# Row skewness of a 1024 x 8192 matrix: part of the cubes on GpSimd, squares in PSUM from block 5 on, new unit sizes

## The chip, the cores and the metric

The kernel runs on one NeuronCore of a Trainium2 chip. The metric is the device time of one launch in microseconds (us). Five engines work side by side, each through its own queue in order: TensorE (PE; PEld is its weight load), VectorE (DVE), ScalarE (ACT), GpSimd (POOL) and SyncE (SP), which here issues the transfers. SBUF is the working memory of 128 partitions; PSUM is the smaller memory into which TensorE writes.

## The reference: the third standardized moment of each row

```python
mean = np.mean(x, axis=-1, keepdims=True)
std = np.std(x, axis=-1, keepdims=True)
z = (x - mean) / (std + 1e-8)
return np.mean(z ** 3, axis=-1).astype(np.float32)
```

x has 1024 rows of 8192 float32 values, 33.55 MB. The kernel reads it once and takes, for each row, the sums of x, of x squared and of x cubed. With m1, m2 and m3 the means of the three, the variance is m2 - m1^2, and the result is (m3 - 3 m1 m2 + 2 m1^3) times the variance to the power -1.5. It is computed as (m3 - 3 m1 (variance + m1^2 / 3)) times that power.

## The kernel before: how the work is cut and ordered

**Tiling.** The rows are 8 blocks (b from 0 to 7), each of one row per partition. The 8192 columns of a block are cut into units, which the table `UNITS` lists; (7,3) below is unit 3 of block 7. Each unit is one transfer (L130) into one of 8 buffers of the pool "xp", whatever its width. There are 31 units. The transfer of a unit waits until the unit eight places earlier has been read by all who read it.

**What is done with a unit.**
- Plain sums: TensorE transposes the unit in chunks of 128 columns and adds all chunks of a block up in one PSUM tile `tp` (L134). At the end of a block, ScalarE copies `tp` to SBUF as `tsb` (L164, for the last block L140), and a matmul with a column of 1/8192 (L165) adds up the 128 partitions, which gives the block's 128 row means, in column b of the PSUM tile `s1ps`.
- Squares: ScalarE squares a slice of the unit and its accumulator gives the slice's sum of squares (L146; in the profile a row ACTIVATE and a short row ACTIVATION_READ_ACCUMULATOR). The squares go to SBUF (pool "sqp", 4 buffers). From unit `PSUM_FROM` = (6,5) on they go to PSUM (pool "psq", 2 buffers).
- Cubes: VectorE multiplies the squares by x and its accumulator gives the sum of cubes (L150). Where the squares lie in SBUF, the product overwrites them. Where they lie in PSUM, it goes to one scratch tile `cube` that all such instructions share.

**Closing.** Blocks 0 to 6 are closed while block 7 is still being worked on, after the unit `EARLY_AT` = (7,2): ScalarE copies the means out of PSUM (L157) and takes three small functions of them (L113 to L115), VectorE adds up the slices' sums (L108), GpSimd does six small steps (L117 to L122). Block 7 is closed at the end: ScalarE copies `tp` (L140) before it squares the last unit, TensorE makes the means (L165), GpSimd and ScalarE take the variance and its power (L172 to L177, the power is L175), VectorE adds up the cubes (L178), joins (L179, L182), and one transfer writes the result (L183).

**Order.** The schedule is manual: each engine executes its instructions in the order in which the code above issues them. Waits between engines follow from the tiles that instructions read and write; an instruction that reads a tile of PSUM written by an earlier one waits for it. Nothing reorders a queue.

Of the kernel before, what the change touches and what calls it, by code (L numbers as in the profile page):

```python
# [8 lines left out]
FP = mybir.dt.float32  # L9
AF = mybir.ActivationFunctionType  # L10
ALU = mybir.AluOpType
# [3 lines left out]
UNITS = [  # L15
    [4096, 4096],
    [4096, 4096],
    [3456, 1792, 2944],
    [2944, 2304, 2944],
    [2944, 2688, 2560],  # L20
    [1920, 1920, 1792, 1536, 1024],
    [1536, 1408, 1408, 1152, 1408, 1280],
    [1152, 1280, 1408, 1280, 1280, 1280, 512],
]
PSUM_FROM = (6, 5)
SUB_MAX = 2304
PS_MAX, PS_BUFS = 1536, 2
X_BUFS = 8
SQ_BUFS = 4
EARLY = 7  # L30
EARLY_AT = (7, 2)


def _slices(w, most):
    n = -(-w // most)
    step = -(-w // n // 128) * 128
    return [(s, min(s + step, w)) for s in range(0, w, step)]


def _plan(b, k):  # L40
    return _slices(UNITS[b][k], PS_MAX if (b, k) >= PSUM_FROM else SUB_MAX)


@with_exitstack
def kernel(
    ctx: ExitStack,
    tc: tile.TileContext,
    x: bass.AP,
    out: bass.AP,
):  # L50
    nc = tc.nc
    eng = mybir.EngineType
    ctx.enter_context(tc.manual_schedule(
        engines={eng.PE, eng.Activation, eng.DVE, eng.Pool, eng.SP}))
    P = nc.NUM_PARTITIONS
    R, C = x.shape
    NB = R // P
    L = NB - 1
    F = EARLY
    inv_n = 1.0 / float(C)  # L60
    s_scale = float(C) ** -0.5
    third = (1.0 / 3.0) ** 0.5
    assert len(UNITS) == NB and all(sum(u) == C for u in UNITS) and F == L


    xv = x.rearrange("(p b) c -> b p c", b=NB)
    ov = out.rearrange("(p b) -> p b", b=NB)


    n_sl = [sum(len(_plan(b, k)) for k in range(len(u))) for b, u in enumerate(UNITS)]  # L70
    K = max(n_sl)

    xpool = ctx.enter_context(tc.tile_pool(name="xp", bufs=X_BUFS))
    sqpool = ctx.enter_context(tc.tile_pool(name="sqp", bufs=SQ_BUFS))
    onep = ctx.enter_context(tc.tile_pool(name="onep", bufs=1))
    psq = ctx.enter_context(tc.tile_pool(name="psq", bufs=PS_BUFS, space=bass.MemoryType.PSUM))
    psum1 = ctx.enter_context(tc.tile_pool(name="ps1", bufs=1, space=bass.MemoryType.PSUM))

    def small(name, n):
        return onep.tile([P, n], FP, tag=name, name=name)  # L80

    onesn = small("onesn", 1)
    nc.vector.memset(onesn, inv_n)  # L83
    tiny = small("tiny", 1)
    nc.scalar.activation(out=tiny, in_=onesn, func=AF.Square)  # L85
    ident = small("ident", P)
    make_identity(nc, ident)
    s2u = small("s2u", NB * K)
    s3u = small("s3u", NB * K)
    nc.vector.memset(s2u, 0.0)  # L90
    nc.vector.memset(s3u, 0.0)
    cube = small("cube", PS_MAX)
    junk = small("junk", K)
    expo = small("expo", F)
    nc.gpsimd.memset(expo, -1.5)
    skew = small("skew", NB)
    m1a = small("m1a", F)
    tsb = small("tsb", P)

    tp = psum1.tile([P, P], FP, tag="tp", name="tp")  # L100
    s1ps = psum1.tile([P, NB], FP, tag="s1ps", name="s1ps")
    act, g = nc.scalar.activation, nc.gpsimd

    def close_first_blocks():

        m2, m3 = small("m2a", F), small("m3a", F)
        for dst, src in ((m2, s2u), (m3, s3u)):
            nc.vector.tensor_reduce(  # L108
                out=dst, in_=src[:, 0 : F * K].rearrange("p (b c) -> p b c", c=K),
                axis=X_AXIS, op=ALU.add,  # L110
            )
        m1sq, m1sq3, nm1 = small("m1sqa", F), small("m1sq3a", F), small("nm1a", F)
        act(out=m1sq, in_=m1a, func=AF.Square)  # L113
        act(out=m1sq3, in_=m1a, func=AF.Square, scale=third)
        act(out=nm1, in_=m1a, func=AF.Copy, scale=-3.0)  # L115
        var, rr = small("vara", F), small("rra", F)
        g.tensor_tensor(out=var, in0=m2, in1=m1sq, op=ALU.subtract)  # L117
        g.tensor_tensor(out=m1sq3, in0=m1sq3, in1=var, op=ALU.add)
        g.tensor_tensor(out=m1sq3, in0=m1sq3, in1=nm1, op=ALU.mult)
        g.tensor_tensor(out=m3, in0=m3, in1=m1sq3, op=ALU.add)  # L120
        g.tensor_tensor(out=rr, in0=var, in1=expo, op=ALU.pow)  # L121
        g.tensor_tensor(out=skew[:, 0:F], in0=m3, in1=rr, op=ALU.mult)  # L122

    for b, widths in enumerate(UNITS):
        c0 = 0
        j = b * K
        for k, w in enumerate(widths):
            last_unit = b == L and k == len(widths) - 1
            xt = xpool.tile([P, w], FP, tag="x", name=f"x_{b}_{k}")
            nc.sync.dma_start(out=xt, in_=xv[b, :, c0 : c0 + w])  # L130
            c0 += w
            n = w // P
            for c in range(n):
                nc.tensor.matmul(  # L134
                    out=tp, lhsT=xt[:, c * P : (c + 1) * P], rhs=ident,
                    start=(k == 0 and c == 0), stop=(c0 == C and c == n - 1),
                    is_transpose=True,
                )
            if last_unit:
                nc.scalar.copy(out=tsb, in_=tp)  # L140
            for s, e in _plan(b, k):
                if (b, k) >= PSUM_FROM:
                    sq = psq.tile([P, PS_MAX], FP, tag="psq", name=f"psq_{b}_{k}_{s}")[:, 0 : e - s]
                else:
                    sq = sqpool.tile([P, e - s], FP, tag="sq", name=f"sq_{b}_{k}_{s}")
                act(  # L146
                    out=sq, in_=xt[:, s:e], func=AF.Square, scale=s_scale,
                    accum_out=s2u[:, j : j + 1],
                )
                nc.vector.scalar_tensor_tensor(  # L150
                    out=cube[:, 0 : e - s] if (b, k) >= PSUM_FROM else sq,
                    in0=sq, scalar=1.0, in1=xt[:, s:e],
                    op0=ALU.mult, op1=ALU.mult, accum_out=s3u[:, j : j + 1],
                )
                j += 1
            if (b, k) == EARLY_AT:
                nc.scalar.copy(out=m1a, in_=s1ps[:, 0:F])  # L157
                close_first_blocks()
            if b == L and k == len(widths) - 2:
                m2p = small("m2p", 1)  # L160
                act(out=junk[:, 0 : n_sl[L] - 1], in_=s2u[:, L * K : j], func=AF.Copy,
                    accum_out=m2p)
        if b < L:
            nc.scalar.copy(out=tsb, in_=tp)  # L164
        nc.tensor.matmul(out=s1ps[:, b : b + 1], lhsT=tsb, rhs=onesn, start=True, stop=True)  # L165


    p1 = s1ps[:, L : L + 1]
    m1sq, nm1, v3, m2, var, rr, num = (
        small(f"{t}_l", 1) for t in ("m1sq", "nm1", "v3", "m2", "var", "rr", "num")  # L170
    )
    g.tensor_tensor(out=m2, in0=m2p, in1=s2u[:, j - 1 : j], op=ALU.add)  # L172
    act(out=m1sq, in_=p1, func=AF.Square)
    g.tensor_tensor(out=var, in0=m2, in1=m1sq, op=ALU.subtract)  # L174
    g.tensor_tensor(out=rr, in0=var, in1=expo[:, 0:1], op=ALU.pow)  # L175
    act(out=nm1, in_=p1, func=AF.Copy, scale=-3.0)
    act(out=v3, in_=m1sq, func=AF.Identity, scale=1.0 / 3.0, bias=var)  # L177
    nc.vector.tensor_reduce(out=num, in_=s3u[:, L * K : L * K + n_sl[L]], axis=X_AXIS, op=ALU.add)  # L178
    nc.vector.scalar_tensor_tensor(  # L179
        out=num, in0=v3, scalar=nm1, in1=num, op0=ALU.mult, op1=ALU.add  # L180
    )
    nc.vector.tensor_tensor(out=skew[:, L:NB], in0=num, in1=rr, op=ALU.mult)  # L182
    nc.sync.dma_start(out=ov, in_=skew)  # L183
# [30 lines left out]
```

## Time and profile before

| what | us |
|---|---|
| median of 3 runs (lowest and highest) | 92.29 (92.27 to 92.38) |
| the profiled execution | 92.38 |
| its span, first to last instruction | 90.6 |
| VectorE busy | 74.1 |
| ScalarE busy | 69.1 |
| TensorE busy | 66.5 |
| GpSimd busy | 4.2 |

The difference between the profiled execution's time and its span, 1.8 us, lies around the span. A row of the profile gives the engine, the line, the operation, output and inputs by the program's names, the shapes, and times in us (a mean in ns). In brackets stands the idle time of the engine just before, and who ended it. A matmul's end is modelled; successive transposes overlap. The granted TensorE clock of the core was 0.99.

### The profile page before, as it was taken

How to read it: one execution, taken by the hardware profiler on the slowest of the kernel's cores; microseconds unless marked ns; L12 is line 12 of the kernel's file. 1: busy time of each engine (PE TensorE's matmuls, PEld its weight loads, DVE VectorE, ACT ScalarE, POOL GpSimd, SP SyncE). 2: the span in 40 equal slices, each digit the busy share in tenths (PEclk: the TensorE clock that was granted, in tenths of full speed). 3: DMA queues.
4: the chain of work that ended last, by engine and by line, in shares of the span. 5: the costliest groups of instructions: out<-in, count | busy, mean ns of one | idle time of the engine just before them, and what ended most of it. 6: DMA issues, size and time to landing. Idle time of an engine off the chain costs nothing. (4 is left out here: it accounts for less than half of the span.)

```text
span 90.6 us, 1442 instructions
## 1 busy us (share of the span) xinstructions
PE 66.5 (73%) x528; PEld 60.2 (66%) x528; DVE 74.1 (82%) x92; ACT 69.1 (76%) x103; POOL 4.2 (5%) x16
## 2 busy tenths in 40 slices
PE   0003999988986959897589778989898798897700
PEld 0003999887975949686569667978687586776600
DVE  0000498969999799999988999999999989989980
ACT  6003969497885979897589889989888798898910
POOL 3000000000000000000000000000000000006440
PEclk9999999999999999999999999999999999999996
DMA  3999999999999999999999999999999999992000
GB/s 101 347 412 427 441 427 420 434 449 430 397 407 442 419 432 426 420 428 418 422 421 433 411 426 411 409 410 420 411 416 420 409 411 421 412 397 115 0 0 2
DMA packets 4614, 33.64 MB, mean 371 GB/s; under 512 B 640, under 2 KB 640, under 8 KB 3072
## 3 DMA queue, kind: packets, MB, share of 16 engines
q1 hardware_dynamic: 4608, 33.56, 89.4%
q8 instruction: 4, 0.07, 0.3%
q14 instruction: 2, 0.02, 0.0%
HBM read 33.55 MB, written 0.00 MB: 370 GB/s over the span
## 5 line engine op out<-in xcount | busy, mean ns | idle before, releaser
L134 PE MATMUL tp<-ident,x 128*128 128x128 f32 x512 | 64.0, 282 | 16.0 <-DMA x<-in_x_dram 15.8
L150 DVE SCALAR_TENSOR_TENSOR sq<-sq,x 128x2048 f32<-128x2048 f32 (+9 forms) x34 | 62.0, 1872 | 12.4 <-ACT sq L146 12.3
L134 PEld LDWEIGHTS tp<-ident,x 128*128 128x128 f32 x512 | 58.3, 146 | 20.3 <-DMA x<-in_x_dram 11.9
L146 ACT ACTIVATE sq<-x 128x2048 f32<-128x2048 f32 (+9 forms) x34 | 53.5, 1575 | 14.4 <-DMA x<-in_x_dram 12.6
L150 DVE SCALAR_TENSOR_TENSOR cube<-psq,x 128x1280 f32<-128x1280 f32 (+3 forms) x8 | 11.1, 1390 | 0.7 <-ACT psq L146 0.2
L146 ACT ACTIVATE psq<-x 128x1280 f32<-128x1280 f32 (+3 forms) x8 | 9.3, 1161 | 0.9 <-DVE cube L150 0.5
L146 ACT ACTIVATION_READ_ACCUMULATOR sq<-x 128x1 f32 x34 | 6.3, 186 | 0.0
L165 PEld LDWEIGHTS s1ps<-onesn,tsb 128*128 128x128 f32 x16 | 2.4, 188 | 5.2 <-ACT tsb L164 4.7
L165 PE MATMUL s1ps<-onesn,tsb 128*128 128x1 f32 x16 | 3.1, 260 | 3.4 <-ACT tsb L164 3.0
L117 POOL TENSOR_TENSOR vara<-m2a,m1sqa 128x7 f32<-128x7 f32 x1 | 0.2, 206 | 80.8 <-DVE m3a L108 80.8
L150 DVE DVE_READ_ACCUMULATOR sq<-sq,x 128x1 f32 x34 | 2.8, 82 | 0.0
L164 ACT COPY tsb<-tp 128x128 f32<-128x128 f32 x7 | 1.7, 250 | 1.3 <-PE tp L134 1.2
L85 ACT ACT_TABLE_LOAD x1 | 1.3, 1283 | 0.7 <-PEq L198 0.7
L121 POOL TENSOR_TENSOR rra<-vara,expo 128x7 f32<-128x7 f32 x1 | 1.5, 1507 | 0.0
L146 ACT ACTIVATION_READ_ACCUMULATOR psq<-x 128x1 f32 x8 | 1.5, 188 | 0.0
L83 DVE MEMSET onesn<- 128x1 f32 x1 | 0.1, 59 | 0.8 <-PEq L198 0.8
L150 DVE DVE_READ_ACCUMULATOR cube<-psq,x 128x1 f32 x8 | 0.7, 84 | 0.0
L177 ACT ACTIVATE v_l<-m1sq_l,var_l 128x1 f32<-128x1 f32 x1 | 0.3, 294 | 0.4 <-POOL var_l L174 0.4
L175 POOL TENSOR_TENSOR rr_l<-var_l,expo 128x1 f32<-128x1 f32 x1 | 0.6, 563 | 0.1
L179 DVE SCALAR_TENSOR_TENSOR num_l<-v_l,nm_l,num_l 128x1 f32<-128x1 f32 x1 | 0.2, 220 | 0.1
masks.py:199 POOL TENSOR_SCALAR_AFFINE_SELECT ident<-ident 128x128 f32<-128x128 f32 x1 | 0.3, 294 | 0.1
L140 ACT COPY tsb<-tp 128x128 f32<-128x128 f32 x1 | 0.3, 266 | 0.0
(27 smaller groups left out, 4.5 us busy)
## 6 DMA issues: line engine op xcount, KB each, us to landing
x<-in_x_dram SPq DMA_DIRECT2D x4, 2048.0 KB, 14.1
x<-in_x_dram SPq DMA_DIRECT2D x4, 1472.0 KB, 27.2
x<-in_x_dram SPq DMA_DIRECT2D x5, 640.0 KB, 9.3
x<-in_x_dram SPq DMA_DIRECT2D x4, 704.0 KB, 10.1
x<-in_x_dram SPq DMA_DIRECT2D x2, 960.0 KB, 19.8
x<-in_x_dram SPq DMA_DIRECT2D x2, 896.0 KB, 22.6
x<-in_x_dram SPq DMA_DIRECT2D x1, 1728.0 KB, 25.4
x<-in_x_dram SPq DMA_DIRECT2D x2, 768.0 KB, 15.2
```

The lines of the kernel that those rows point to most:

```text
L85: nc.scalar.activation(out=tiny, in_=onesn, func=AF.Square)
L117: g.tensor_tensor(out=var, in0=m2, in1=m1sq, op=ALU.subtract)
L121: g.tensor_tensor(out=rr, in0=var, in1=expo, op=ALU.pow)
L134: nc.tensor.matmul(out=tp, lhsT=xt[:, c * P : (c + 1) * P], rhs=ident, start=(k == 0 and c == 0), stop=(c0 == C and c == n - 1), is_transp ...
L140: nc.scalar.copy(out=tsb, in_=tp)
L146: act(out=sq, in_=xt[:, s:e], func=AF.Square, scale=s_scale, accum_out=s2u[:, j : j + 1],)
L150: nc.vector.scalar_tensor_tensor(out=cube[:, 0 : e - s] if (b, k) >= PSUM_FROM else sq, in0=sq, scalar=1.0, in1=xt[:, s:e], op0=ALU.mult, ...
L164: nc.scalar.copy(out=tsb, in_=tp)
L165: nc.tensor.matmul(out=s1ps[:, b : b + 1], lhsT=tsb, rhs=onesn, start=True, stop=True)
L175: g.tensor_tensor(out=rr, in0=var, in1=expo[:, 0:1], op=ALU.pow)
L177: act(out=v3, in_=m1sq, func=AF.Identity, scale=1.0 / 3.0, bias=var)
L179: nc.vector.scalar_tensor_tensor(out=num, in0=v3, scalar=nm1, in1=num, op0=ALU.mult, op1=ALU.add)
```

## The change

Five things change together.

- `UNITS` is cut anew, still 31 units: block 2 gets two large units, block 7 gets nine units, seven of 1024 to 896 columns and then 768 and 384.
- The first 1024 columns of the units (6,0), (7,0) and (7,2) get their cubes from GpSimd (`POOL`). (7,0) and (7,2) are 1024 columns wide and are done wholly there; of (6,0), 512 columns stay on VectorE. ScalarE squares into a tile `gsq` in SBUF (2 buffers), and GpSimd multiplies it by x in place.
- GpSimd's product has no accumulator here, so the cubes are added up as the plain sums are, by the new `sum_cubes`: TensorE transposes eight chunks into one PSUM tile, ScalarE copies it to SBUF, a matmul with a column of ones follows, and ScalarE copies the result into the slice's place in `s3u`. The three steps are issued after the third, fourth and fifth unit that follow.
- Squares go to PSUM from unit (5,3) on, in slices of at most 1024 columns and with 3 buffers, instead of from (6,5) on with at most 1536 and 2.
- The PSUM tile `s1ps` becomes a part of a tile `misc`, which also holds the transposed cubes (`gps`) and their sums. `EARLY_AT` is now (7,3). In the built program, the copy of the means (in the old code L157) waits until TensorE has finished the transposes of the cubes of (7,0), which are issued just before it.

```diff
 UNITS = [
     [4096, 4096],
     [4096, 4096],
-    [3456, 1792, 2944],
-    [2944, 2304, 2944],
-    [2944, 2688, 2560],
-    [1920, 1920, 1792, 1536, 1024],
-    [1536, 1408, 1408, 1152, 1408, 1280],
-    [1152, 1280, 1408, 1280, 1280, 1280, 512],
+    [4096, 4096],
+    [3584, 2560, 2048],
+    [3072, 2816, 2304],
+    [2816, 1664, 2176, 1536],
+    [1536, 1920, 1920, 1024, 896, 896],
+    [1024, 1024, 1024, 1024, 1024, 1024, 896, 768, 384],
 ]
-PSUM_FROM = (6, 5)
+POOL = {(6, 0): 1024, (7, 0): 1024, (7, 2): 1024}
+PSUM_FROM = (5, 3)
 SUB_MAX = 2304
-PS_MAX, PS_BUFS = 1536, 2
+PS_MAX, PS_BUFS = 1024, 3
...
-EARLY_AT = (7, 2)
+EARLY_AT = (7, 3)
...
 def _plan(b, k):
-    return _slices(UNITS[b][k], PS_MAX if (b, k) >= PSUM_FROM else SUB_MAX)
+
+    w, g = UNITS[b][k], POOL.get((b, k), 0)
+    most = PS_MAX if (b, k) >= PSUM_FROM else SUB_MAX
+    return ([(0, g, True)] if g else []) + [(g + s, g + e, False) for s, e in _slices(w - g, most)]
...
+    gpool = ctx.enter_context(tc.tile_pool(name="gp", bufs=2))
...
+    ones = small("ones", 1)
+    nc.gpsimd.memset(ones, 1.0)
...
+    gsb = small("gsb", P)
...
-    s1ps = psum1.tile([P, NB], FP, tag="s1ps", name="s1ps")
+    misc = psum1.tile([P, 2 * P], FP, tag="misc", name="misc")
+    gps = misc[:, 0:P]
+    s1ps = misc[:, P : P + NB]
...
+    def sum_cubes(sq, col):
+
+        n = sq.shape[1] // P
+        for c in range(n):
+            nc.tensor.matmul(
+                out=gps, lhsT=sq[:, c * P : (c + 1) * P], rhs=ident,
+                start=c == 0, stop=c == n - 1, is_transpose=True,
+            )
+        yield
+        nc.scalar.copy(out=gsb, in_=gps)
+        p3 = misc[:, P + NB : P + NB + 1]
+        nc.tensor.matmul(out=p3, lhsT=gsb, rhs=ones, start=True, stop=True)
+        yield
+        nc.scalar.copy(out=s3u[:, col : col + 1], in_=p3)
...
-            for s, e in _plan(b, k):
-                if (b, k) >= PSUM_FROM:
+            for s, e, on_pool in _plan(b, k):
+                if on_pool:
+                    sq = gpool.tile([P, e - s], FP, tag="gsq", name=f"gsq_{b}_{k}")
+                elif (b, k) >= PSUM_FROM:
...
-                nc.vector.scalar_tensor_tensor(
-                    out=cube[:, 0 : e - s] if (b, k) >= PSUM_FROM else sq,
-                    in0=sq, scalar=1.0, in1=xt[:, s:e],
-                    op0=ALU.mult, op1=ALU.mult, accum_out=s3u[:, j : j + 1],
-                )
+                if on_pool:
+                    g.tensor_tensor(out=sq, in0=sq, in1=xt[:, s:e], op=ALU.mult)
+                    steps = sum_cubes(sq, j)
+                    later += [(i + 3, steps), (i + 4, steps), (i + 5, steps)]
+                else:
+                    nc.vector.scalar_tensor_tensor(
+                        out=cube[:, 0 : e - s] if (b, k) >= PSUM_FROM else sq,
+                        in0=sq, scalar=1.0, in1=xt[:, s:e],
+                        op0=ALU.mult, op1=ALU.mult, accum_out=s3u[:, j : j + 1],
+                    )
                 j += 1
+            for at, steps in later:
+                if at == i:
+                    next(steps, None)
+            later = [z for z in later if z[0] > i]
             if (b, k) == EARLY_AT:
                 nc.scalar.copy(out=m1a, in_=s1ps[:, 0:F])
                 close_first_blocks()
...
+            i += 1
```

Here i counts units through all blocks, so the steps for (7,0) come after (7,3), (7,4) and (7,5), and those for (7,2) after (7,5), (7,6) and (7,7).

## The prediction

> **What bounds the kernel now.** I read the page first: engine shares, then its slices.
>
> ```profile
> span 90.6 us, 1442 instructions
> PE 66.5 (73%) x528; PEld 60.2 (66%) x528; DVE 74.1 (82%) x92; ACT 69.1 (76%) x103; POOL 4.2 (5%) x16
> ...
> PEclk9999999999999999999999999999999999999996
> DMA  3999999999999999999999999999999999992000
> ```
>
> The DMA row is what fills the span: its slices stand at 9 up to about 81 us, while no engine is busy for more than 82%. Loading sets the pace. TensorE's clock is full throughout. So what can be won or lost lies in how long the work goes on after the transfers, in the last ten us. The second view is the chain that ended last, in order of time; it names the engine that finishes last.
>
> ```profile
> 86.80 0.71 DVE cube L150 x2
> 87.51 0.02 issue
> 87.54 0.17 DVE num_l L178
> ...
> 88.14 0.16 DVE skew L182
> ```
>
> The chain is VectorE's alone. The third view is the timeline of the last ten us (start, duration, engine, line, operation; in brackets the idle time before it).
>
> ```profile
> 80.14 0.14 ACT L157 COPY m1a<-s1ps 128x7 f32<-128x7 f32 x1
> 80.31 1.31 PE L134 MATMUL tp<-ident,x 128*128 128x128 f32 x10 [0.17 <-DMA x<-in_x_dram]
> 80.62 1.22 ACT L146 ACTIVATE psq<-x 128x1280 f32<-128x1280 f32 x1
> 82.04 1.48 DVE L150 SCALAR_TENSOR_TENSOR cube<-psq,x 128x1280 f32<-128x1280 f32 x1
> 83.41 1.75 PE L134 MATMUL tp<-ident,x 128*128 128x128 f32 x14 [0.23 <-DMA x<-in_x_dram]
> 83.62 1.49 DVE L150 SCALAR_TENSOR_TENSOR cube<-psq,x 128x1280 f32<-128x1280 f32 x1
> 85.19 0.27 ACT L140 COPY tsb<-tp 128x128 f32<-128x128 f32 x1
> 85.21 1.49 DVE L150 SCALAR_TENSOR_TENSOR cube<-psq,x 128x1280 f32<-128x1280 f32 x1
> 85.36 0.61 ACT L146 ACTIVATE psq<-x 128x512 f32<-128x512 f32 x1
> 85.51 0.30 PEld L165 LDWEIGHTS s1ps<-onesn,tsb 128*128 128x128 f32 x2 [0.59 <-ACT tsb L140]
> 85.98 0.16 ACT L173 ACTIVATE m1sq_l<-s1ps 128x1 f32<-128x1 f32 x1
> 86.70 0.56 POOL L175 TENSOR_TENSOR rr_l<-var_l,expo 128x1 f32<-128x1 f32 x1
> 86.80 0.69 DVE L150 SCALAR_TENSOR_TENSOR cube<-psq,x 128x512 f32<-128x512 f32 x1
> 88.14 0.16 DVE L182 TENSOR_TENSOR skew<-num_l,rr_l 128x1 f32<-128x1 f32 x1
> ```
>
> VectorE takes one 1280-column cube every 1.58 to 1.59 us (82.04, 83.62, 85.21, 86.80), as long as such a unit takes to arrive (TensorE started on them at 80.31 and 83.41: two units in 3.10). It is about a unit behind and cannot catch up. A second path ends earlier: the copy of the sums at 85.19, the matmul, ScalarE's square at 85.98, GpSimd's steps, the power done at 86.70 + 0.56 = 87.26. The last operation, at 88.14, could have taken it 0.88 us sooner. So VectorE decides, with 0.88 us of room before the copy at 85.19 would.
>
> **The change part by part.**
>
> *Transfers.* 31 before and after, same bytes. In these rows a unit of 1280 columns takes 1.55 to 1.59 us, 1.21 to 1.24 us per 1000. I take the landing of any given column as unmoved by the new cuts. Unit (7,3) leaves 4096 columns to come; in the kernel before, unit (7,3), where TensorE starts at 80.31, leaves 3072. The 1024 columns between are 1.24 to 1.27 us: TensorE starts on the new (7,3) at 79.0. On SyncE's queue two transfers now wait for a GpSimd cube before their buffer is free, that of (7,2) for (6,0) and the last one for (7,0), whose end I put at 79.1 at the latest; the first transfer of all, issued at 0.74, let TensorE start at 8.29 with 4096 columns, so one of 384 needs some 3 us (7.55 less 3712 columns at 1.22), and it is wanted at 84. Hidden until GpSimd ends after 81.
>
> *VectorE.* It loses 3072 columns, 1.04 ns each (the 1408- and 512-column rows, 1625 and 691 ns, differ by 934 over 896): 3.2 us. Squares in PSUM cost it something: 1280 columns take 1.58 from start to start with the shared scratch tile as output, against 1.42 with squares in SBUF (54.02, 55.43, 56.85); 19 such instructions instead of 8 give back 1.8, and there are 43 cubes in place of 42 (0.16 more). With nothing to do for (7,0) and (7,2) it is level with ScalarE by (7,3). From there 1024 columns take 0.157 + 1.067 + 0.10 = 1.32.
>
> *GpSimd's cubes.* No such row exists. The nearest are its own products: 203 ns at 7 columns, 192 at 1, so 1.83 ns per column, 2.06 us for 1024. Ends: the 128-column memset against the one-column ones (205 and 99) gives 0.83 ns, 1.0 us; the affine select's 294 ns over 128 columns gives 2.3 ns, 2.35 us. I take 2.06. Its (7,0) square can be done between 76.3 and 77.0: the data land at 75.1, but ScalarE first copies block 6's sums, which wait for TensorE. It ends by 79.1, and its consumer stands behind (7,3) on TensorE, at 79.0 + 0.05 + 8 x 0.109 = 79.92. Hidden with 0.8 to spare; past that, every us is paid.
> A rule speaks against this part: the Trainium skill's "GPSIMD Engine Reference", section 4.1, says to do elementwise products on VectorE and not on GpSimd, about half as fast. Its section 3.1 gives 4497 ns for 2048 columns; halved, an estimate of 2.25 us where the rows give 2.06, and the sum stays as it is. No run shown here has such a product.
>
> *TensorE.* Three groups of eight transposes and three small matmuls are new. Transposes follow each other at 0.109 (14 in 1.75, the last of 0.273), so each group is 0.87 and a small matmul 0.14 of queue (weights at 85.51, two loads in 0.30). Two groups and two small matmuls fall behind (7,3): 2.0 us in a stretch where the queue had 0.2 to 0.5 us idle per unit.
>
> *The added waits.* ScalarE's copy of the first seven means now reads a tile that also holds the transposed cubes. By the order of the instructions it waits for the group of (7,0), which stands on TensorE behind (7,3). Queued behind it on ScalarE: three small operations and the square of (7,4). And the small matmul of (7,0) stands ahead of the transposes of (7,5), waiting for ScalarE's copy of the cubes, which stands behind the square of (7,4). Step by step: TensorE from 79.0, 0.05 for the first weights, 16 x 0.109, free 80.80, last result 80.96; copy at 80.99; the next square 0.48 later (80.14 to 80.62), 81.47, although (7,4) is there at 80.25. It takes 1.03 (0.83 ns per column between 607 and 1349 ns). Copy of the cubes 82.51, done 82.78; small matmul 82.82, transposes of (7,5) from 82.96, though landed at 81.5. Behind them the group of (7,2), then (7,6): 23 x 0.109, 85.47; small matmul, 85.61; nine more, 86.59, last result 86.75; copy of the sums 86.78. That is 1.59 after 85.19. Minus the 0.88 of room, plus 0.04 for the signal: +0.75.
>
> *VectorE then* gets (7,4) at 82.6 and takes 1.32, 1.32, 1.19, 1.06: its last cube could start at 87.5, but the square of (7,8), 0.50 long from 86.95, is done with its accumulator at 87.6. Last cube 0.56, end of sums near 88.4, level with the other path (last operation 88.89). ScalarE's six extra copies (0.11 to 0.16 of queue each) and four extra squares (0.18 of fixed time each, what is left of the 607 ns after 512 columns) lie inside these waits and the idle time before (7,3); without that cover they would be 1.5 us. The ones tile and the wider clears cost nothing: start-up ends by 2.3 us, the first data come at 8.2.
>
> *Sum.* The profiled execution took 92.38 with its span of 90.6; 92.38 + 0.75 = 93.13. It is the slowest of the runs shown; from their median, 92.29, it is 93.04. I say 93.05. The path is good to 0.3 or so either way: 92.7 to 93.4.
>
> **Rivals.**
> *The relief reaches the end: faster.* If the waits cost TensorE nothing, its queue from 79.0 holds 56 transposes and two small matmuls: 0.05 + 6.10 + 0.28, free 85.43, copy of the sums 85.62, 0.43 late, inside the 0.88 of room. VectorE would get (7,4) at 81.45 and start its last cube at 86.34 instead of 86.80. The last operation comes at 87.73, 0.41 earlier: 91.9. For it: TensorE idled at every unit of the timeline. Against: the order on two queues that I followed. It decides when TensorE loses under 0.4 us in these waits, where I count 1.16. Chance 0.2; a loss near 0.4, no change within 0.2% (0.18 us, what a measurement can tell), 0.1.
> *GpSimd is slow.* If its two reads share a path with VectorE's and 1024 columns take 4.1 us, (7,0) ends at 81.1, 1.2 after it is wanted, and (7,2) at 85.2, about 0.3 after its own delayed place: 93.05 + 1.5 = 94.5. For: no large product of it is in the trace. Against: VectorE reads one operand from PSUM by then. Chance 0.12.
> *The last transfers come later.* The chain hangs on the landing of (7,3). Landings can shift by 0.3 with other unit sizes; were it 1 us, 94.05. For: DMA has no idle time to absorb it. Against: same bytes. Chance 0.05.
>
> **How the numbers follow.** Forecast 0.53 (92.7 to 93.4), faster 0.2, same 0.1, the two slow rivals 0.17. Faster 0.2, same 0.1, slower 0.7. The range runs from the faster rival to the later transfers, 91.8 to 94.2; outside it lies most of the slow GpSimd case and little else.
>
> **What would show it.** Right: the copy of the means waits 0.5 to 1 us on TensorE; the small matmul near 82.8 waits on ScalarE; the copy of the sums near 86.8; the chain that ended last leaves VectorE's row of cubes; GpSimd's products 1.8 to 2.4 us each. Wrong: TensorE keeps up with the landings after (7,3), VectorE starts the last cube before 86.5, or GpSimd's products exceed 2.8 us.

## Result and profile after

The changed kernel takes 93.33 us (median of 4 runs, 93.24 to 93.47), the kernel before 92.34 in the same comparison (92.27 to 92.40). The ratio is 1.0109, with a 95% interval of 1.0092 to 1.0127: it is slower by about 1.0 us. The forecast was 93.05, slower, in a range of 91.8 to 94.2. The profiled execution took 93.47 against 92.38 before, with a span of 91.6 against 90.6.

The page of the changed kernel first: the span, the busy times, and the two rows of slices.

```profile
span 91.6 us, 1528 instructions
PE 68.9 (75%) x558; PEld 64.8 (71%) x558; DVE 71.7 (78%) x94; ACT 70.1 (76%) x117; POOL 11.3 (12%) x20
...
DVE  1000498989899398999999999998999999668970
...
DMA  4899999999999999999999999999999999980000
```

VectorE is busy for 2.4 us less and GpSimd for 7.1 us more, as the change says. VectorE's row has a hole near the end (66), which it did not have before:

```profile
DVE  0000498969999799999988999999999989989980
```

The DMA row ends where it ended before, to within a slice. The busy times by stretch say it more exactly; first the kernel before, then the changed one (us of the stretch, its length, busy time and instructions of each engine, TensorE's clock, DMA's share, GB/s).

```profile
79.00:84.00 5.00, 4.36 (x36) 3.64 (x35) 4.68 (x9) 4.70 (x11) 1.60 (x5) 1.00 0.64 254
84.00:88.40 4.40, 1.54 (x13) 1.22 (x11) 3.86 (x9) 2.47 (x10) 1.83 (x5) 1.00 0.00 0
```

```profile
79.00:84.00 5.00, 3.99 (x37) 3.76 (x35) 3.27 (x8) 4.23 (x15) 4.76 (x7) 1.00 0.64 250
84.00:89.40 5.40, 3.53 (x31) 3.12 (x29) 4.44 (x13) 3.66 (x15) 1.69 (x5) 1.00 0.00 0
```

The transfers end alike: the same DMA share from 79 to 84 us, none after it. Before 84 VectorE and ScalarE are busy for less time than in the kernel before, and TensorE has begun only one instruction more (37 against 36), although the transposes of the cubes were added to its queue; after 84, TensorE has 3.53 us left in place of 1.54. Work that could have been done before the last landing was held up and is done after it. The chain that ended last shows by what (start, duration, engine, output, line):

```profile
80.22 0.89 PE misc L140 x8
...
81.13 0.17 ACT m1a L197
...
81.73 1.04 ACT psq L177 x2
82.77 0.16 ACT gsb L145
...
82.97 0.38 PE misc L147 x2
83.35 0.93 PE tp L163 x8
84.29 0.94 PE misc L140 x8
85.22 0.76 PE tp L163 x7
85.99 0.12 PE misc L147 x2
86.10 1.05 PE tp L163 x9
...
88.53 0.30 ACT v_l L219
```

It is the chain of the prediction, link by link: transposes of GpSimd's cubes of (7,0) (L140), the copy of the means (L197), the square of (7,4) (L177), the copy of the cubes (L145), their small matmul (L147), then TensorE's queue with hardly a gap up to the last transposes, and from there the closing of block 7. VectorE's cubes, which were the chain before, are not in it. The timeline of the same kernel has the idle times:

```profile
77.36 4.71 POOL L182 TENSOR_TENSOR gsq<-gsq,x 128x1024 f32<-128x1024 f32 x2 [7.96 <-ACT gsq L177]
79.95 0.91 PEld L140 LDWEIGHTS misc<-ident,gsq 128*128 128x128 f32 x8
81.13 0.17 ACT L197 COPY m1a<-misc 128x7 f32<-128x7 f32 x1 [0.73 <-PE misc L140]
81.64 1.01 ACT L177 ACTIVATE psq<-x 128x1024 f32<-128x1024 f32 x1
82.80 1.23 DVE L186 SCALAR_TENSOR_TENSOR cube<-psq,x 128x1024 f32<-128x1024 f32 x1 [0.89 <-ACT psq L177]
82.97 0.30 PEld L147 LDWEIGHTS misc<-ones,gsb 128*128 128x128 f32 x2 [1.24 <-ACT gsb L145]
83.21 1.07 PE L163 MATMUL tp<-ident,x 128*128 128x128 f32 x8
87.18 0.27 ACT L169 COPY tsb<-tp 128x128 f32<-128x128 f32 x1 [0.43 <-PE tp L163]
88.00 0.56 DVE L186 SCALAR_TENSOR_TENSOR cube<-psq,x 128x384 f32<-128x384 f32 x1 [0.39 <-ACT psq L177]
89.20 0.16 DVE L224 TENSOR_TENSOR skew<-num_l,rr_l 128x1 f32<-128x1 f32 x1
```

ScalarE waits 0.73 us for the means, TensorE's weight load 1.24 us for the cubes, VectorE 0.89 us for the square. The copy of the last sums comes at 87.18 where it came at 85.19, 1.99 later; 0.88 of that was free, and the last operation is at 89.20 where it was at 88.14.

### The profile page after: what moved, and what is told of

It reads as the page before. It is cut to its first block, busy times and chain, and to the rows that moved or that the text cites. A ratio compares the mean times of both kernels' runs of the same rounds, so it can differ in the third digit from the quotient of the medians.

```text
span 91.6 us, 1528 instructions
## 1 busy us (share of the span) xinstructions
PE 68.9 (75%) x558; PEld 64.8 (71%) x558; DVE 71.7 (78%) x94; ACT 70.1 (76%) x117; POOL 11.3 (12%) x20
## 4 chain that ended last, share of the span: by engine, by line
DMA 65%; PE 18%; ACT 5%; DVE 5%; issue 2%; SPq 1%; POOL 0%; ACTq 0%; DVEq 0%
DMA x<-in_x_dram 65%; PE tp L163 14%; DVE sq L186 5%; PE misc L140 3%; ACT sq L177 2%; ACT psq L177 2%; SPq L159 1%; PE misc L147 1%; PE misc L206 0%; ACT v_l L219 0%; ACT tsb L205 0%; DVE num_l L221 0%; POOL var_l L216 0%; POOL m_l L214 0%; ACT nm1a L127 0%
## 5 line engine op out<-in xcount | busy, mean ns | idle before, releaser
L186 DVE SCALAR_TENSOR_TENSOR sq<-sq,x 128x2048 f32<-128x2048 f32 (+7 forms) x26 | 52.4, 2064 | 13.0 <-ACT sq L177 13.0
L177 ACT ACTIVATE sq<-x 128x2048 f32<-128x2048 f32 (+7 forms) x26 | 44.8, 1725 | 14.0 <-DMA x<-in_x_dram 14.0
L186 DVE SCALAR_TENSOR_TENSOR cube<-psq,x 128x1024 f32<-128x1024 f32 (+4 forms) x17 | 18.2, 1068 | 3.5 <-ACT psq L177 2.4
L182 POOL TENSOR_TENSOR gsq<-gsq,x 128x1024 f32<-128x1024 f32 x3 | 7.1, 2375 | 73.6 <-ACT gsq L177 73.6
L177 ACT ACTIVATE psq<-x 128x1024 f32<-128x1024 f32 (+4 forms) x17 | 15.2, 893 | 0.8 <-DMA x<-in_x_dram 0.8
L206 PEld LDWEIGHTS misc<-onesn,tsb 128*128 128x128 f32 x16 | 2.4, 188 | 5.5 <-ACT tsb L205 4.9
L206 PE MATMUL misc<-onesn,tsb 128*128 128x1 f32 x16 | 3.1, 260 | 3.6 <-ACT tsb L205 3.2
L177 ACT ACTIVATION_READ_ACCUMULATOR sq<-x 128x1 f32 x26 | 4.8, 185 | 0.0
L177 ACT ACTIVATION_READ_ACCUMULATOR psq<-x 128x1 f32 x17 | 3.2, 189 | 0.0
L177 ACT ACTIVATE gsq<-x 128x1024 f32<-128x1024 f32 x3 | 3.2, 1054 | 0.0
L140 PE MATMUL misc<-ident,gsq 128*128 128x128 f32 x24 | 3.1, 274 | 0.0
L140 PEld LDWEIGHTS misc<-ident,gsq 128*128 128x128 f32 x24 | 2.7, 141 | 0.1
L147 PEld LDWEIGHTS misc<-ones,gsb 128*128 128x128 f32 x6 | 0.9, 189 | 1.4 <-ACT gsb L145 1.4
L147 PE MATMUL misc<-ones,gsb 128*128 128x1 f32 x6 | 1.0, 244 | 1.0 <-ACT gsb L145 1.0
L145 ACT COPY gsb<-misc 128x128 f32<-128x128 f32 x3 | 0.8, 251 | 0.4 <-PE misc L140 0.4
```

Source lines behind the costliest of these rows:

```text
L140: nc.tensor.matmul(out=gps, lhsT=sq[:, c * P : (c + 1) * P], rhs=ident, start=c == 0, stop=c == n - 1, is_transpose=True,)
L145: nc.scalar.copy(out=gsb, in_=gps)
L147: nc.tensor.matmul(out=p3, lhsT=gsb, rhs=ones, start=True, stop=True)
L177: act(out=sq, in_=xt[:, s:e], func=AF.Square, scale=s_scale, accum_out=s2u[:, j : j + 1],)
L182: g.tensor_tensor(out=sq, in0=sq, in1=xt[:, s:e], op=ALU.mult)
L186: nc.vector.scalar_tensor_tensor(out=cube[:, 0 : e - s] if (b, k) >= PSUM_FROM else sq, in0=sq, scalar=1.0, in1=xt[:, s:e], op0=ALU.mult, ...
```

## The experiments

All times are medians; each ratio is to the kernel before, measured on the same chip, with its 95% interval.

### 1. Is it the waits, or the work added to TensorE?

Four kernels each undo one part of the change, and a fifth joins two of the edits. The first moves the closing of the first seven blocks, and with it the copy of the means, ahead of the transposes of GpSimd's cubes.

```diff
-EARLY_AT = (7, 3)
+EARLY_AT = (7, 2)
```

> One edit to the changed kernel: the first seven blocks are closed after unit (7,2) again, so the copy of the means stands ahead of the transposes of GpSimd's cubes of (7,0) and waits for nothing. Theory (the time is lost in the wait of the copy of the means, 1.17 us on ScalarE in the trace: square of (7,4) at 81.64 for data landed at 80.24): the square of (7,4) starts near 80.5, the copy of the last sums near 86.3 instead of 87.18, time 92.5 (92.3 to 92.7). Rival (the transposes added to TensorE are the loss, whatever waits): 93.2 to 93.4, no change. Rival (VectorE's small slices from PSUM are the loss): no change either, 93.3.

Measured: 92.38 us, ratio 1.0018 (1.0006 to 1.0029). One place in the order is worth 0.95 us by the medians and 0.84 by the ratios (1.0109 to 1.0018; the kernel before took 92.29 here, 92.34 there), most of the loss. The timeline of this kernel:

```profile
79.01 0.15 ACT L197 COPY m1a<-misc 128x7 f32<-128x7 f32 x1
81.58 0.24 ACT L145 COPY gsb<-misc 128x128 f32<-128x128 f32 x1
81.88 0.30 PEld L147 LDWEIGHTS misc<-ones,gsb 128*128 128x128 f32 x2 [0.40 <-ACT gsb L145]
86.09 0.27 ACT L169 COPY tsb<-tp 128x128 f32<-128x128 f32 x1 [0.43 <-PE tp L163]
```

The copy of the means waits for nothing. The small matmul comes 1.09 us earlier and so does the copy of the sums (86.09 against 87.18): what is won up to the small matmul arrives at the last link. Of the 1.09 us, 0.25 were there before the edit could act (the transposes of (7,0)'s cubes begin at 79.70, in the changed kernel at 79.95): in this execution the data landed earlier. The other 0.84 is what the ratios say too. TensorE has exactly the same instructions as in the changed kernel, so their number alone is not what made it slower. The wait comes from the tile that the means share with the transposed cubes; a tile of their own for the means would be another way out of it, and was not run.

The second and the third take steps of `sum_cubes` away.

```diff
         yield
-        nc.scalar.copy(out=gsb, in_=gps)
-        p3 = misc[:, P + NB : P + NB + 1]
-        nc.tensor.matmul(out=p3, lhsT=gsb, rhs=ones, start=True, stop=True)
         yield
-        nc.scalar.copy(out=s3u[:, col : col + 1], in_=p3)
```

> The changed kernel without the second and third step of the sums of GpSimd's cubes: no copy of the transposed cubes, no small matmul, no copy into s3u; the cubes of the three slices are left out of the result. The transposes and the wait of the means stay. Theory (the small matmul waits for ScalarE ahead of the transposes of (7,5), 1.0 us of TensorE idle in the trace, but the square of (7,4) stays late by the first wait): a gain of 0.3 to 0.5, 92.9 (92.7 to 93.1). Rival (transposes are the loss): 93.2 or more. Rival (the small matmul's wait is the whole loss): 92.3.

Measured: 92.88 us, ratio 1.0065 (1.0049 to 1.0081): 0.45 us less than the changed kernel (0.41 by the ratios), with the wait of the means still there. The timeline of this kernel:

```profile
80.65 0.17 ACT L193 COPY m1a<-misc 128x7 f32<-128x7 f32 x1 [0.81 <-PE misc L140]
85.33 0.24 ACT L165 COPY tsb<-tp 128x128 f32<-128x128 f32 x1
87.22 0.56 DVE L182 SCALAR_TENSOR_TENSOR cube<-psq,x 128x384 f32<-128x384 f32 x1
```

TensorE's copy of the sums is 1.85 us earlier than in the changed kernel, but the time gains far less, because VectorE now decides the end: its cubes are late by the squares that stand behind the copy of the means. So the wait of the means delays two paths, TensorE's and VectorE's, and the wait of the small matmul mainly the first.

```diff
-                    later += [(i + 3, steps), (i + 4, steps), (i + 5, steps)]
```

> The changed kernel without any of the three steps: GpSimd still makes its three products, but nobody adds them up; their cubes are left out of the result. Theory (all of the loss comes from the sums on TensorE and the waits they make): below the kernel before, 92.0 (91.7 to 92.2), TensorE waits for landings again after (7,3), VectorE decides the end. Rival (VectorE's small slices from PSUM, or the new unit sizes, are the loss): 93.0 to 93.4.

Measured: 91.85 us, ratio 0.9958 (0.9941 to 0.9974). Without the sums the rest of the change is a gain of 0.4 us. The timeline shows TensorE waiting for landings again and VectorE deciding the end:

```profile
81.34 3.23 PE L163 MATMUL tp<-ident,x 128*128 128x128 f32 x24 [0.18 <-DMA x<-in_x_dram]
84.60 0.27 ACT L169 COPY tsb<-tp 128x128 f32<-128x128 f32 x1
86.43 0.56 DVE L185 SCALAR_TENSOR_TENSOR cube<-psq,x 128x384 f32<-128x384 f32 x1
87.63 0.16 DVE L223 TENSOR_TENSOR skew<-num_l,rr_l 128x1 f32<-128x1 f32 x1
```

The last operation stands 0.51 us ahead of where it stood before (88.14). This is the gain that the relief of VectorE, with the new sizes and the squares in PSUM, would have brought if the sums had cost nothing.

Both edits of the first two together (closing after (7,2), transposes alone) show whether the two waits are one:

> The changed kernel with both: the first seven blocks closed after (7,2), and of the sums of GpSimd's cubes only the transposes (their cubes are left out of the result). Theory (the two waits are separate: the copy of the means 0.95, the small matmuls with their copies 0.45, and the bare transposes cost next to nothing): 92.0 (91.8 to 92.2), 0.1 to 0.2 above the kernel without the sums. Rival (the two waits are one chain, either edit ends it): 92.4, as with the early closing alone. Rival (transposes cost by themselves): 92.4 or more.

Measured: 92.07 us, ratio 0.9976 (0.9966 to 0.9986). The four values form a square: 93.33, 92.38 with the first wait gone, 92.88 with the small matmuls and copies gone, 92.07 with both. The first edit is worth 0.95 or 0.81, the second 0.45 or 0.31. By the ratios, which take out that the kernel before drifted between 92.34 and 92.26, it is 0.84 or 0.82 and 0.41 or 0.39, so the two losses add up. What is left against the kernel without sums, 0.22 us (0.17 by the ratios), comes with the bare transposes; the two kernels also differ in the place of the closing, which waits for nothing in either. So the sums cost 1.4 us in all (0.84, 0.39 and 0.17), the rest of the change gains 0.4, and 1.0 remains.

The fourth gives GpSimd nothing.

```diff
-POOL = {(6, 0): 1024, (7, 0): 1024, (7, 2): 1024}
+POOL = {}
```

> The changed kernel with no slice given to GpSimd: all cubes on VectorE, in slices of at most 1024 from PSUM; nothing is left out. Theory (VectorE's period of 1.32 us for 1024 columns from PSUM is longer than the 1.27 in which they arrive, and 3072 columns more are 3.9 us on it, of which it can make up some): 95.0 (94.5 to 95.5), VectorE without a gap from about 70 us on. Rival (VectorE is relieved for nothing, the sums on TensorE are the only thing that counts): 92.0 as without the sums.

Measured: 95.01 us, ratio 1.0298 (1.0282 to 1.0313). The relief by GpSimd is needed in this kernel: without it VectorE, at 1.32 us for 1024 columns, is the bound by far. GpSimd's part as a whole, sums included, wins 1.7 us there.

### 2. The other two parts: unit sizes and squares in PSUM

The kernel before with the new table `UNITS`, nothing else:

> The kernel before with the new unit sizes alone: no GpSimd, squares in PSUM from (6,5) as before. Theory (seventeen small units instead of thirteen at the end cost VectorE a fixed 0.26 us each when squares are in PSUM, and nothing relieves it): 93.4 (93.0 to 93.8), VectorE without a gap from about (7,0) on. Rival (smaller units at the end shorten the work after the last landing): below 92.2.

Measured: 93.27 us, ratio 1.0104 (1.0086 to 1.0121). The new sizes alone cost 1.0 us. From 73 us on VectorE goes from cube to cube, and ScalarE waits for a buffer. The time is as expected, but the fixed cost of small units is the smaller part of it. Here is VectorE at unit (6,1), with 14848 columns left in both kernels, first in the kernel before, then with the new sizes:

```profile
69.17 1.62 DVE L150 SCALAR_TENSOR_TENSOR sq<-sq,x 128x1408 f32<-128x1408 f32 x1
```

```profile
69.95 2.16 DVE L150 SCALAR_TENSOR_TENSOR sq<-sq,x 128x1920 f32<-128x1920 f32 x1
```

It is already 0.78 us late: the new units of block 5 are wider, and so is (6,1) itself. At the end the last operation is 1.06 late (89.20 against 88.14). That the wider units make it late is read from the two traces, and no run separates it. The new cuts are therefore not good by themselves; they need the relief.

Squares in SBUF in the changed kernel (the slices then go up to 2304 columns again):

```diff
-PSUM_FROM = (5, 3)
+PSUM_FROM = (9, 0)
```

> The changed kernel with every square in SBUF (in place, as the first blocks have it), so that VectorE reads two operands from SBUF beside GpSimd's products, which read two as well. Theory (TensorE's chain decides, VectorE has room, and nothing is lost between the two engines): 93.3 (93.0 to 93.5), GpSimd's products stay at 2.37 us, VectorE's 1024-column cubes at 1.23. Rival (the two engines share a way to SBUF, and the second to start waits, as the Trainium skill's page on SBUF has it for two SBUF inputs): GpSimd's products 3 us and more or VectorE's cubes beside them over 2 us, time 94 to 96.

Measured: 96.78 us, ratio 1.0484 (1.0466 to 1.0502). The theory that nothing is lost between the two engines fell. The rival's account holds (a product of 3.58 us, cubes of over 2 us), though its time, 94 to 96, was too low. The timeline of this kernel around GpSimd's first product:

```profile
66.30 1.76 DVE L186 SCALAR_TENSOR_TENSOR sq<-sq,x 128x1536 f32<-128x1536 f32 x1
66.71 3.58 POOL L182 TENSOR_TENSOR gsq<-gsq,x 128x1024 f32<-128x1024 f32 x1 [65.32 <-ACT gsq L177]
67.97 2.86 DVE L186 SCALAR_TENSOR_TENSOR sq<-sq,x 128x512 f32<-128x512 f32 x1
...
80.28 3.37 DVE L186 SCALAR_TENSOR_TENSOR sq<-sq,x 128x1024 f32<-128x1024 f32 x1
83.58 1.21 DVE L186 SCALAR_TENSOR_TENSOR sq<-sq,x 128x1024 f32<-128x1024 f32 x1
...
85.07 1.18 POOL L129 TENSOR_TENSOR vara<-m2a,m1sqa 128x7 f32<-128x7 f32 x1 [2.51 <-DVE m3a L120]
...
91.31 0.19 POOL L214 TENSOR_TENSOR m_l<-m2p,s2u 128x1 f32<-128x1 f32 x1
```

GpSimd's product is issued while a cube of VectorE runs and takes 3.58 us in place of 2.37: it ends 2.2 us after that cube. The next cube, of only 512 columns, begins meanwhile and takes 2.86 us, ending at 70.83, 0.54 us after the product. A cube of 1024 columns takes 3.37 us beside a product and 1.21 alone. Whichever comes second stands still until the first is all but through. That is what the Trainium skill's "SBUF — State Buffer", section "Who interferes with whom", says of a VectorE instruction with two SBUF inputs beside a GpSimd instruction that reads SBUF, and the trace agrees: after the first was through, the second still needed 2.2 of its 2.37 us, or 0.54 of its 0.69. In the changed kernel, where VectorE reads one operand from PSUM, its 1024-column cubes take 1.23 us beside GpSimd's product and without it. The loss reaches the end through GpSimd's closing of the first seven blocks: it begins at 85.07, in the changed kernel at 82.02, because VectorE's cubes stood still; its six steps take 6.3 us in place of 2.8, because they stand still in turn; and block 7's first step comes at 91.31 in place of 88.04.

### 3. What VectorE pays with squares in PSUM

The kernel before, with three scratch tiles in turn:

```diff
-    cube = small("cube", PS_MAX)
+    cubes = [small(f"cube{q}", PS_MAX) for q in range(3)]
...
-                    out=cube[:, 0 : e - s] if (b, k) >= PSUM_FROM else sq,
+                    out=cubes[j % 3][:, 0 : e - s] if (b, k) >= PSUM_FROM else sq,
```

> The kernel before with three scratch tiles for the cubes in turn instead of one; nothing else. Theory (the cube with squares in PSUM takes 1.59 us from start to start against 1.42 in SBUF because each waits for the one before it to have written the shared scratch tile): 1280-column cubes follow at 1.42 to 1.45, the last cube starts near 86.4 instead of 86.80, 91.9 (91.7 to 92.1). Rival (the read from PSUM itself is what is slower): spacing stays at 1.59, 92.3.

Measured: 91.89 us, ratio 0.9951 (0.9935 to 0.9966).

```profile
82.05 1.48 DVE L150 SCALAR_TENSOR_TENSOR cube<-psq,x 128x1280 f32<-128x1280 f32 x1
83.46 1.49 DVE L150 SCALAR_TENSOR_TENSOR cube<-psq,x 128x1280 f32<-128x1280 f32 x1
86.39 0.69 DVE L150 SCALAR_TENSOR_TENSOR cube<-psq,x 128x512 f32<-128x512 f32 x1
```

Two cubes follow at 1.41 us (82.05, 83.46) where the kernel before had 1.58 (82.04, 83.62), with the same duration of 1.48 to 1.49. Not the read from PSUM is slower; each cube waited for the one before it to have written the shared tile, whose contents nobody reads.

With no scratch tile at all, because all squares lie in SBUF, and a finer end:

```diff
-    [1152, 1280, 1408, 1280, 1280, 1280, 512],
+    [1280, 1280, 1152, 1024, 1024, 1024, 896, 512],
...
-PSUM_FROM = (6, 5)
+PSUM_FROM = (9, 0)
```

> The kernel before with all squares in SBUF and block 7 in eight units, 1280, 1280, 1152, 1024, 1024, 1024, 896, 512: no scratch tile, so VectorE's period is short, and less work is left after each landing. Theory (as for the three scratch tiles; the fixed cost per unit is then small enough for small units): last cube near 85.9, the variance's path and VectorE level at the end, 91.5 (91.3 to 91.8). Rival (small units cost VectorE as much as in the kernel with the new sizes alone): 92.3 or more.

Measured: 93.75 us, ratio 1.0152 (1.0129 to 1.0175), a miss by 2.2 us. VectorE did nearly what was expected, its last cube starts at 86.16 and its last sum is at 86.89. GpSimd did not; its timeline in this kernel:

```profile
81.84 1.16 POOL L117 TENSOR_TENSOR vara<-m2a,m1sqa 128x7 f32<-128x7 f32 x1 [80.48 <-DVE m3a L108]
83.07 1.06 POOL L118 TENSOR_TENSOR m1sq3a<-m1sq3a,vara 128x7 f32<-128x7 f32 x1
...
85.36 0.94 POOL L120 TENSOR_TENSOR m3a<-m3a,m1sq3a 128x7 f32<-128x7 f32 x1
...
88.46 0.19 POOL L172 TENSOR_TENSOR m_l<-m2p,s2u 128x1 f32<-128x1 f32 x1
```

Sums and products of seven columns, 0.20 us in the kernel before and in the changed kernel, take 0.94 to 1.16, as they did in the kernel above: each stands still for a cube of VectorE. The closing of block 7 begins at 88.46, where it began at 86.16 before. So it pays to have the squares in PSUM at the end even where GpSimd is given no cubes.

### 4. Two versions that are faster than both kernels

The changed kernel with closing after (7,2), GpSimd's slice of (7,2) given back, and three scratch tiles:

```diff
-POOL = {(6, 0): 1024, (7, 0): 1024, (7, 2): 1024}
+POOL = {(6, 0): 1024, (7, 0): 1024}
...
-EARLY_AT = (7, 3)
+EARLY_AT = (7, 2)
...
(three scratch tiles as above)
```

> The changed kernel with the first seven blocks closed after (7,2), GpSimd's cubes of (7,2) given back to VectorE, and three scratch tiles in turn. Theory (the group of (7,2) and its small matmul were the last load that kept TensorE's copy of the sums late; VectorE, without the wait on the scratch tile, can take these cubes): 91.6 (91.4 to 91.9). Rival (VectorE needs the relief): 92.3 or more.

Measured: 91.54 us, ratio 0.9922 (0.9906 to 0.9937). These three edits were not run one by one on this kernel.

The kernel before with three scratch tiles, the finer end, and PSUM from (7,3) on, when GpSimd begins to close blocks:

```diff
-    [1152, 1280, 1408, 1280, 1280, 1280, 512],
+    [1280, 1280, 1152, 1024, 1024, 1024, 896, 512],
...
-PSUM_FROM = (6, 5)
+PSUM_FROM = (7, 3)
...
-PS_MAX, PS_BUFS = 1536, 2
+PS_MAX, PS_BUFS = 1024, 3
...
(three scratch tiles as above)
```

> The kernel before with three scratch tiles in turn and block 7 in eight units, 1280, 1280, 1152, 1024, 1024, 1024, 896, 512; squares in PSUM only from (7,3) on, three buffers of 1024 columns, so that they lie there while GpSimd closes blocks. No cube is given to GpSimd. Theory (the loss with all squares in SBUF came from GpSimd's closing steps being held up beside VectorE; in PSUM they take 0.2 us each again, and the small end then pays): 91.5 (91.3 to 91.8), GpSimd's first closing step 0.21 us. Rival (small units cost VectorE as much as they save at the end): 91.9 or more, no better than three scratch tiles alone.

Measured: 91.63 us, ratio 0.9922 (0.9905 to 0.9938).

```profile
81.91 0.21 POOL L117 TENSOR_TENSOR vara<-m2a,m1sqa 128x7 f32<-128x7 f32 x1 [80.55 <-DVE m3a L108]
86.23 0.69 DVE L150 SCALAR_TENSOR_TENSOR cube<-psq,x 128x512 f32<-128x512 f32 x1
86.69 0.56 POOL L175 TENSOR_TENSOR rr_l<-var_l,expo 128x1 f32<-128x1 f32 x1
```

GpSimd's first step takes 0.21 us again. The last cube (86.23) and the power (86.69 + 0.56) now end within 0.4 us of each other. The two versions do not differ measurably, so 0.7 us can be had with GpSimd's cubes or without them.

## Why the prediction was right

*Direction and path.* The predicted chain is the measured one, and undoing its first link (experiment 1, closing after (7,2)) gives back 0.95 of the 0.99 us by the medians, five sixths of the loss by the ratios.

*Size.* I had +0.75 us for the last operation; it is +1.06 (88.14 to 89.20). The terms, predicted and measured: transposes of (7,0)'s cubes 79.92, weights at 79.95; copy of the means 80.99, 81.13; square of (7,4) 81.47, 81.64; small matmul 82.82, 82.97; copy of the last sums 86.78, 87.18; from there to the last operation 2.11, 2.02. Up to the small matmul the path was 0.15 us short, and the stretch after it 0.25 (3.96 predicted, 4.21 measured). A tenth of that is at the first small matmul: I counted 0.14 us until the transposes behind it, and the trace has 0.24 (82.97 to 83.21); the second took its 0.15. Another tenth lies in the 23 transposes between the two, 2.61 us where I counted 2.51; TensorE waited there on a semaphore for 0.05 us, at 84.1 before the cubes of (7,2), and the trace does not say for what. Such tenths are no more than the landings vary by: TensorE begins unit (6,2) at 70.37 in this execution, and between 69.98 and 70.33 in the executions of experiments 1 and 2 with the same units.

*Two readings of the prediction are wrong.* The row beside the 0.109 us between transposes gives 0.114, (1.75 - 0.273) / 13; 0.109 is nearer to the changed kernel's groups (eight in 1.04, 0.110). With 0.114 the path would have come out some 0.2 us longer, nearer to what was measured. And 17 cubes have their squares in PSUM, not 19, so they give back 1.4 us of the relief and not 1.8; that is no term of the path.

*TensorE at (7,3).* I let it wait for the landing at 79.0. It was already behind: it went through the transposes of (7,0) to (7,3) without an idle time longer than 0.1 us. That the start of the group came out right was luck: the two times were nearly equal.

*GpSimd.* I took 2.06 us from its rows of 1 and 7 columns, with an upper end of 2.35; it is 2.37. Extrapolation from so small a shape was 13% short. The estimate by the Trainium skill's "GPSIMD Engine Reference", section 3.1, was 2.25, nearer. The consequence stood, but with little to spare: the product of (7,0) ends at 79.74, just before its consumer at 79.95, 0.21 us instead of 0.8.

*VectorE.* The spacing of 1.32 us for 1024 columns is what the trace has (82.80, 84.13, 85.45), and its last cube was late by the square it waited for, as said. Its path ends level with the other, also as said: the sums of the cubes are ready at 88.76, the variance's last term at 88.82. Its cost per cube with squares in PSUM was right in size; the cause, the shared tile, was only shown by the three scratch tiles.

*Transfers.* They ended as before; the rival in which they come later did not happen. Nor did the rival of a slow GpSimd, but experiment 2 shows that it was real: had the squares of the last blocks been in SBUF, the two engines would have blocked each other, and 96.78 us would have been outside the range. That VectorE reads one operand from PSUM, the prediction's argument against this rival, was the right one.

*The faster rival.* It was near to what the rest of the change is worth: 91.9 predicted if the waits cost TensorE nothing, 91.85 measured without the sums. The two conditions differ, so the agreement is in part luck: the rival kept the transposes in TensorE's queue, and with them in it and both waits gone 92.07 was measured.

## What to carry to other kernels

When work is moved from a busy engine to an idle one, follow what the result has to pass through on its way back: here the product was hidden, and the sum of it on two in-order queues was not. Before a small operation is put into a queue, ask what it will wait for and what large work stands behind it; one unit earlier for the copy of seven means was worth 0.84 to 0.95 us with not one instruction less. Look for outputs that nobody reads: a shared scratch tile makes each instruction wait for the last one.

## What the runs showed of the hardware that I had not expected

- When GpSimd and VectorE both read two operands from SBUF, the second to come does hardly anything until the first is through (it still needed 2.2 of 2.37 us, 0.54 of 0.69), and small operations suffer most: 0.20 us became 0.94 to 1.16, and 512 columns on VectorE took 2.86 us in place of 0.69.
- A VectorE instruction whose output tile is also the output of the one before it costs 0.17 us more from start to start (1.58 against 1.41 at 1280 columns), with the same duration in the profile.
- On TensorE, the first transpose behind a small matmul starts 0.24 us after the small matmul's weights (82.97 to 83.21), where transposes follow each other at 0.11; its own weights start 0.13 after them (83.10).
